# First-group scores over 128 rows, value products two blocks at a time, scores last in a slot

## The chip, the cores and the metric

The kernel runs on one core of one Trainium2 chip. The metric is the device time of one execution in microseconds (us); for several runs their median is given. A profile is one execution recorded by the hardware profiler. Engines are PE (TensorE matmul; its weight loads have a row of their own, PEld), DVE (VectorE), ACT (ScalarE), POOL (GpSimd) and SP (SyncE, which issues most DMAs).

## The reference

Two layers over a sequence of 512 rows of 1024 floats. Each layer normalises, projects to queries, keys and values of three dilated attention groups (8 heads of 64), pools, gates, merges, and ends with a SwiGLU FFN. What matters here is the attention:

```python
scores = jnp.einsum('bhnqd,bhnkd->bhnqk', qb, kw).astype(jnp.float32) * (Dh ** -0.5)
scores = scores - slopes.astype(jnp.float32)[:, None, None, None] * dist[None, None]
scores = jnp.where(valid, scores, -1e30)
lse = jax.nn.logsumexp(scores, axis=-1)
p = jnp.exp(scores - lse[..., None])
out = jnp.einsum('bhnqk,bhnkd->bhnqd', p.astype(vw.dtype), vw)
...
wts = jax.nn.softmax(jnp.stack(lses, axis=0), axis=0)
att = jnp.sum(wts[..., None].astype(x.dtype) * jnp.stack(outs, axis=0), axis=0)
```

Queries see keys at most 64 steps away; the three groups step by 1, 4 and 16 positions.

## The kernel before

Float32 products are made of float32r parts: a value is split into a high part (a rounded copy, made by ACT) and a low part (the difference, made by DVE), and `mm3` (L239 to L241) multiplies high by high, high by low and low by high. A projection (`proj`) is 24 such matmuls of 512 columns, over 8 blocks of the model width, into one bank of PSUM.

The attention is done for a pair of heads at a time (j = 0 to 3, in both layers, 8 attentions). `qk(l, j)` makes six projections q0, k0, q1, k1, q2, k2, and calls `slot()` before each of them. A slot runs what is due of earlier work: deferred functions, then one step of each attention that is open (`self.attn`, oldest first), then one step of the adaLN weights (`ada_run`, one weight load and one DVE product, L205). Attention j is opened when its six projections are done, so its steps run between the projections of j + 1; those of the last pair run between the gate projections (`gates`), where a slot stands ahead of 36 matmuls. All engines take their instructions in the order in which the code issues them; nothing is planned by due times. So what a slot issues stands ahead of the next projection in PE's queue, and ahead of that projection's eviction and of the next weight splits (L198 on ACT, L199 on DVE) in the other queues.

An attention works on four blocks. Blocks 0 and 1 are the first group, each of two tiles of 128 queries; blocks 2 and 3 hold the second and third group side by side. The steps are these functions:

- `scores(blk)`: into the two PSUM banks "s". For blocks 0 and 1 there are 8 matmuls of 256 columns. The query tile of a head holds the high part on its own 64 rows and the low part on the other 64; `ks[h]` holds the head's key high part on both halves of the rows. So L541 (128 rows) gives high by high and low by high in one matmul, and L542 (the 64 rows of the query's high part, with the key's low part in `ks[2]`, both heads in one tile) adds high by low. For blocks 2 and 3 `mm3` is used with 12 matmuls of 256 columns and 128 rows. Then for each of four pieces a DVE reduction (L559) adds the distance table and takes the minimum, and an ACT exponential (L563) with that minimum as bias gives the weights and their sum.
- `transposes(blk)`: transposes the weights on PE into a bank "pt" (L573 for blocks 0 and 1, eight; L583 for blocks 2 and 3, four, with a DVE transposition L586 for the other half) and copies them out, half by DVE (L575) and half by ACT (L577, L587).
- `values(blk)`: 16 matmuls of 128 columns (L607) into a bank "mm" that the two blocks of a group share.
- `exchange()`: two POOL DMAs (L611, L612) that bring the sums of the first group into the layout of the others. `weigh()` (first instruction L620, DVE) combines the sums, `spread()` transposes the weights (L633) and broadcasts them with POOL DMAs (L637, L640), `combine()` (DVE, L645, L646 and a split) closes the attention two slots later. So the combine of attention j falls into slot 1 of attention j + 1.

Slot by slot before: 0: scores(0). 1: scores(1), transposes(0). 2: scores(2), transposes(1), exchange, values(0). 3: scores(3), transposes(2), values(1). 4: transposes(3), values(2), weigh. 5: values(3), spread. 6: nothing. 7: combine.

`key_tiles` builds the key tiles of the first group: `padded` evicts the projection into a padded tile (ACT L457, DVE L458), `stacked` makes high parts (ACT L465) and low parts (DVE L467), and two POOL copies (L473, L474) fill the other halves of `ks[0]` and `ks[1]`.

Of the kernel before, what the change touches and what calls it, by code (L numbers as in the profile page):

```python
# [12 lines left out]
F32 = mybir.dt.float32  # L13
F32R = mybir.dt.float32r
# [14 lines left out]
P = 128  # L29
# [15 lines left out]
def slope(g, h):  # L45
    return 2.0 ** (-8.0 * (8 * g + h + 1) / 24.0)


class Net:
# [71 lines left out]
    def slot(self):  # L121
        due, keep = [], []
        for e in self.later:
            e[0] -= 1
            (due if e[0] <= 0 else keep).append(e)
        self.later = keep
        for e in due:
            e[1]()
        self.attn = [g for g in self.attn if next(g, True) is None]
        while self.ada:  # L130
            if next(self.ada[0], True) is None:
                break
            self.ada.pop(0)
# [10 lines left out]
        return self.sb.tile(shape, dt, tag=tag, name=self.name(tag), bufs=bufs)  # L144

    def g(self, shape=(P, 2, S), dt=F32):
        return self.t("g", list(shape), dt, 23)

    def bank(self, tag="mm"):
        return self.ps.tile([P, S], F32, tag=tag, name=self.name(tag), bufs={"mm": 4, "s": 2, "pt": 2}[tag])  # L150
# [299 lines left out]

    def padded(self, pb):
        nc = self.nc
        vp = self.t("kp", [P, 5, 8, 16], F32, 4)
        src = pb.rearrange("d (c u t) -> d t u c", c=16, u=8)
        nc.gpsimd.memset(vp[:, 0, 0:4], 0.0)
        nc.gpsimd.memset(vp[:, 4, 4:8], 0.0)
        nc.scalar.copy(vp[:, 0:4, 4:8], src[:, :, 0:4])  # L457
        nc.vector.tensor_copy(vp[:, 1:5, 0:4], src[:, :, 4:8])  # L458
        return vp
# [8 lines left out]

    def key_tiles(self, pb):
        full = self.padded(pb)  # L470
        ks = [self.t("kp", [P, 5, 8, 16], F32R, 4) for _ in range(3)]
        self.stacked(full, ks, (ks[2][0:64], ks[2][64:128]))
        self.nc.gpsimd.tensor_copy(ks[0][64:128], ks[0][0:64].bitcast(F32))  # L473
        self.nc.gpsimd.tensor_copy(ks[1][0:64], ks[1][64:128].bitcast(F32))  # L474
        return ks

    def query_tiles(self, pb, j):
# [43 lines left out]
    def attention(self, j, x, res):  # L521
        nc = self.nc
# [4 lines left out]
        def scores(blk):  # L527
            s, tt = divmod(blk, 2)
            pr[blk] = self.g([P, 2, 2, 256])
            sc = [self.bank("s") for _ in range(2)]  # L530
            for ti in range(2):
                t = 2 * tt + ti
                tk = slice(t * P, t * P + P)
                mm = nc.tensor.matmul
                for h in range(2):
                    if s == 0:
                        hs = slice(64 * h, 64 * h + 64)
                        o = sc[h][:, ti * 256 : ti * 256 + 256]
                        q, ks = x["q0"][:, h, tk], x["k0"]
                        k = lambda z: z[:, t : t + 2].rearrange("d b u c -> d (b u c)")  # L540
                        mm(o, lhsT=q, rhs=k(ks[h]), start=True, stop=False)  # L541
                        mm(o, lhsT=q[hs], rhs=k(ks[2])[hs], start=False, stop=True)  # L542
                    else:
                        o = sc[ti][:, h * 256 : h * 256 + 256]
                        q, ks = x[f"q{h + 1}"], x[f"k{h + 1}"]
                        k = lambda z: z[:, t].rearrange("d h k -> d (h k)")
                        self.mm3(o, q[:, 0, tk], q[:, 1, tk], k(ks[0]), k(ks[1]), True, True)
            for ti in range(2):
                t = 2 * tt + ti
                for h in range(2):  # L550
                    o = pr[blk][:, h, ti]
                    if s == 0:
                        tb, acc = (0 if t == 0 else 2 if t == 3 else 1), sta[:, t, h]
                        i0, i1, o2 = sc[h][:, ti * 256 : ti * 256 + 256], self.tab[:, tb], o
                    else:
                        acc = st[:, 1, t, h]
                        i0 = sc[ti].rearrange("q (g h k) -> q h g k", g=2, h=2)[:, h]
                        i1, o2 = (z.rearrange("q (g k) -> q g k", g=2) for z in (self.tab[:, 3], o))
                    nc.vector.tensor_tensor_reduce(  # L559
                        out=o2, in0=i0, in1=i1, op0=ALU.add, op1=ALU.min,  # L560
                        scale=-slope(s, 2 * j + h), scalar=3e38, accum_out=acc[:, 0:1],
                    )
                    nc.scalar.activation(o, o, AF.Exp, bias=acc[:, 0:1], scale=-1.0, accum_out=acc[:, 1:2])  # L563

        def transposes(blk):
            ptr[blk] = self.g([P, 2, S])
            if blk < 2:
                for h in range(2):
                    pt = self.bank("pt")
                    for ti in range(2):  # L570
                        for b in range(2):
                            c = (2 * ti + b) * P
                            nc.tensor.transpose(pt[:, c : c + P], pr[blk][:, h, ti, b * P : b * P + P], self.ident)  # L573
                    if h:
                        nc.vector.tensor_copy(ptr[blk][:, h], pt)  # L575
                    else:
                        nc.scalar.copy(ptr[blk][:, h], pt)  # L577
            else:
                pt = self.bank("pt")
                for h in range(2):  # L580
                    for ti in range(2):
                        c = (2 * h + ti) * P
                        nc.tensor.transpose(pt[:, c : c + P], pr[blk][:, h, ti, 0:P], self.ident)  # L583
                o = ptr[blk].rearrange("k h (t b q) -> k (h t) b q", t=2, b=2)
                i = pr[blk].rearrange("q h t (b k) -> q (h t) b k", b=2)
                nc.vector.transpose(o[:, :, 1], i[:, :, 1])  # L586
                nc.scalar.copy(o[:, :, 0], pt.rearrange("k (a q) -> k a q", a=4))  # L587

        def values(blk):
            s, tt = divmod(blk, 2)  # L590
            if tt == 0:
                pvs[s] = self.bank()
            pv = pvs[s]
            for ti in range(2):
                t = 2 * tt + ti
                for b in range(2):
                    for h in range(2):
                        hd = (2 * j + h) * HD
                        c = (2 * ti + b) * P
                        rhs = ptr[blk][:, h, c : c + P]  # L600
                        if s == 0:
                            o = pv[64 * h : 64 * h + 64].rearrange("d (c t) -> d t c", t=4)[:, t]
                            v = self.vs[(t + b) // 2][:, (t + b) % 2, hd : hd + HD]
                        else:
                            o = pv[64 * h : 64 * h + 64, t * P : t * P + P]
                            v = self.vb[t][:, b, hd : hd + HD]
                        nc.tensor.matmul(o, lhsT=v, rhs=rhs, start=b == 0, stop=b == 1)  # L607

        def exchange():
            d1 = self.dr.tile([P, 16], F32, tag="d1", name=self.name("d1"), bufs=2)  # L610
            nc.gpsimd.dma_start(out=d1, in_=sta.rearrange("q t h e -> q (t h e)"))  # L611
            nc.gpsimd.dma_start(out=st[:, 0].rearrange("q p h e -> q p (h e)"), in_=d1.rearrange("(p c) (t e) -> (c t) p e", p=4, t=4))  # L612
# [3 lines left out]
        def weigh():  # L616
            nmn = self.t("nmn", [P, 4, 2], F32, 2)
            es = self.t("es", [P, 2, 2, 4], F32, 2)
            z = self.t("z1", [P, 2, 4], F32, 2)
            nc.vector.tensor_tensor(nmn, st[:, 0, :, :, 0], st[:, 1, :, :, 0], op=ALU.min)  # L620
            for s in range(2):
                nc.vector.tensor_sub(wt[:, s], nmn.rearrange("q p h -> q h p"), st[:, s, :, :, 0].rearrange("q p h -> q h p"))
            nc.scalar.activation(wt, wt, AF.Exp)
            for s in range(2):
                nc.vector.tensor_mul(es[:, s], wt[:, s], st[:, s, :, :, 1].rearrange("q p h -> q h p"))
            nc.vector.tensor_add(z, es[:, 0], es[:, 1])
            nc.vector.reciprocal(z, z)
            for s in range(2):
                nc.vector.tensor_mul(wt[:, s], wt[:, s], z)
# [19 lines left out]
            res.append(at)  # L649

        for i in range(4):
            scores(i)
            if i >= 1:
                transposes(i - 1)
            if i == 2:
                exchange()
            if i >= 2:
                values(i - 2)
            yield
        transposes(3)  # L660
        values(2)
        weigh()
        yield
        values(3)
        wb = spread()
        yield
# [354 lines left out]

# [11 lines left out]
```

## Time and profile before

| | us |
|---|---|
| median of 3 runs | 1731.49 (1730.62 to 1733.04) |
| span of the profiled execution | 1732.1 |
| PE busy | 1688.3 |
| DVE busy | 965.5 |
| ACT busy | 658.7 |
| POOL busy | 351.1 |

The profiled execution has no other time of its own: its span, first to last instruction, is 1732.1 us, 0.6 over the median of the runs. PE's busy time is the union of its matmuls' lengths; matmuls overlap, so a busy PE can still be slower or faster in the distance from one start to the next, which the timeline shows. The attentions run from 158 to 360 us in layer 0 and from 1010 to 1211 us in layer 1.

### The profile page before, as it was taken

How to read it: one execution, taken by the hardware profiler on the slowest of the kernel's cores; microseconds unless marked ns; L12 is line 12 of the kernel's file. 1: busy time of each engine (PE TensorE's matmuls, PEld its weight loads, DVE VectorE, ACT ScalarE, POOL GpSimd, SP SyncE). 2: the span in 40 equal slices, each digit the busy share in tenths (PEclk: the TensorE clock that was granted, in tenths of full speed). 3: DMA queues.
4: the chain of work that ended last, by engine and by line, in shares of the span. 5: the costliest groups of instructions: out<-in, count | busy, mean ns of one | idle time of the engine just before them, and what ended most of it. 6: DMA issues, size and time to landing. Idle time of an engine off the chain costs nothing.

```text
span 1732.1 us, 21129 instructions
## 1 busy us (share of the span) xinstructions
PE 1688.3 (97%) x8162; PEld 1384.0 (80%) x8162; DVE 965.5 (56%) x1628; ACT 658.7 (38%) x1110; POOL 351.1 (20%) x317
## 2 busy tenths in 40 slices
PE   7899999999989999999999999999999999999998
PEld 5687788888779888888878887878887888888886
DVE  8657677545685554333473676764367844333435
ACT  4246444633443222221352554446234422222212
POOL 4301221002340000255330021120032400004540
PEclk9999999999999999999999999999999999999999
DMA  7524444332532555332522254452325344322331
GB/s 273 203 73 166 157 136 138 109 113 81 195 110 96 190 195 176 111 108 96 184 110 79 83 173 134 143 162 86 98 98 182 110 146 146 97 98 97 106 138 49
DMA packets 63799, 227.20 MB, mean 131 GB/s; under 512 B 7681, under 2 KB 8097, under 8 KB 63698
## 3 DMA queue, kind: packets, MB, share of 16 engines
q1 hardware_dynamic: 55296, 199.25, 33.9%
q0 software_dynamic: 8400, 26.59, 4.8%
q8 instruction: 64, 1.05, 0.3%
q14 instruction: 37, 0.30, 0.1%
q10 hardware_dynamic: 2, 0.00, 0.0%
HBM read 217.28 MB, written 8.54 MB: 130 GB/s over the span
## 4 chain that ended last, share of the span: by engine, by line
PE 90%; DVE 6%; ACT 2%; issue 1%; DMA 0%; POOL 0%; DVEq 0%
PE mm L239 21%; PE mm L241 20%; PE mm L240 20%; PE mm L775 8%; PE pt L775 5%; PE s L775 4%; PE mm L607 2%; PE mm L389 1%; DVE raw L205 1%; PE pt L389 1%; PE s L542 1%; PE s L541 1%; PE pt L573 1%; DVE nt L260 1%; DVE rs L264 1%
## 5 line engine op out<-in xcount | busy, mean ns | idle before, releaser
L239 PE MATMUL mm<-h,w 128*128 128x512 f32 (+1 forms) x1440 | 560.6, 389 | 0.0
L241 PE MATMUL mm<-h,w 128*128 128x512 f32 (+1 forms) x1440 | 554.6, 385 | 0.0
L240 PE MATMUL mm<-h,w 128*128 128x512 f32 (+1 forms) x1440 | 553.7, 385 | 0.0
L199 DVE TENSOR_TENSOR w<-raw,w 128x1024 fp32r<-128x1024 f32 x238 | 309.8, 1316 | 188.5 <-ACT w L198 188.5
L198 ACT CAST w<-raw 128x1024 fp32r<-128x1024 f32 x254 | 259.8, 1044 | 168.4 <-PE mm L775 141.7
L239 PEld LDWEIGHTS mm<-h,w 128*128 128x128 f32 x1440 | 270.6, 188 | 57.0 <-issue 3.8
L241 PEld LDWEIGHTS mm<-h,w 128*128 128x128 f32 x1440 | 270.6, 188 | 55.4
L240 PEld LDWEIGHTS mm<-h,w 128*128 128x128 f32 x1440 | 270.8, 188 | 52.4
L100 POOL TENSOR_TENSOR raw<-raw,g 128x1024 f32<-128x1024 f32 x60 | 158.2, 2648 | 375.0 <-DMA raw<-w_ffn_out 221.4
L198 ACT CAST g<-g 128x512 fp32r<-128x512 f32 x76 | 47.2, 621 | 336.7 <-DVE g L871 217.0
L775 PE MATMUL mm<-w,g 128*128 128x512 f32 x600 | 147.2, 395 | 0.0
L871 DVE TENSOR_TENSOR g<-g,mm 128x512 f32<-128x512 f32 x42 | 28.9, 688 | 211.4 <-PE mm L241 198.8
L775 PEld LDWEIGHTS mm<-w,g 128*128 128x128 f32 x600 | 112.6, 188 | 27.1
L205 DVE SCALAR_TENSOR_TENSOR raw<-raw,silc 128x1024 f32<-128x1024 f32 x96 | 132.2, 1384 | 1.6 <-DMA raw<-w_ada 1.6
L199 DVE TENSOR_TENSOR g<-g,g 128x512 fp32r<-128x512 f32 x76 | 61.9, 815 | 70.8 <-ACT g L198 70.8
L775 PE MATMUL s<-w,g 128*128 128x512 f32 x300 | 78.9, 403 | 2.1 <-ACT w L198 1.3
L775 PE MATMUL pt<-w,g 128*128 128x512 f32 x300 | 76.3, 395 | 0.0
L775 PEld LDWEIGHTS s<-w,g 128*128 128x128 f32 x300 | 57.5, 193 | 17.1 <-ACT w L198 1.8
L775 PEld LDWEIGHTS pt<-w,g 128*128 128x128 f32 x300 | 56.4, 188 | 13.6
L232 POOL DMA_DIRECT2D dg<-gr x4 | 2.1, 536 | 290.2 <-DVE gr L230 290.2
L473 POOL CAST kp<-kp 64x640 fp32r<-64x640 f32 x8 | 10.9, 1368 | 235.0 <-ACT kp L465 235.0
L870 ACT ACTIVATE g<-mm 128x512 f32<-128x512 f32 x42 | 25.2, 600 | 84.6 <-PE mm L241 84.6
(229 smaller groups left out, 2085.6 us busy)
## 6 DMA issues: line engine op xcount, KB each, us to landing
raw<-w_in SPq DMA_DIRECT2D x112, 512.0 KB, 3.3
raw<-w_ada SPq DMA_DIRECT2D x96, 512.0 KB, 4.3
raw<-w_ffn_in SPq DMA_DIRECT2D x88, 512.0 KB, 3.3
raw<-w_ffn_out SPq DMA_DIRECT2D x44, 512.0 KB, 3.2
raw<-w_o SPq DMA_DIRECT2D x16, 512.0 KB, 4.2
xs<-g POOLq DMA_DIRECT2D x12, 512.0 KB, 2.9
g<-xs POOLq DMA_DIRECT2D x12, 512.0 KB, 5.9
g<-d POOLq DMA_DIRECT2D x16, 256.0 KB, 5.6
```

The lines of the kernel that those rows point to most:

```text
L100: self.nc.gpsimd.tensor_mul(self.raws[i], self.raws[i], self.gate[info(i)][0])
L198: self.nc.scalar.copy(dst_hi, src)
L199: (self.nc.gpsimd if pool else self.nc.vector).tensor_sub(dst_lo, src, dst_hi.bitcast(F32))
L205: self.nc.vector.scalar_tensor_tensor(raw, raw, 1.0, self.silc, op0=ALU.mult, op1=ALU.mult, accum_out=self.mod[:, l, m : m + 1])
L239: mm(out, lhsT=whi, rhs=xhi, start=first, stop=False)
L240: mm(out, lhsT=whi, rhs=xlo, start=False, stop=False)
L241: mm(out, lhsT=wlo, rhs=xhi, start=False, stop=last)
L389: nc.tensor.matmul(pv[p, g], lhsT=hh[:, hi, tk], rhs=w[k][wi][:, c], start=k == 0 and i == 0, stop=k == KD - 1 and i == 2)
L607: nc.tensor.matmul(o, lhsT=v, rhs=rhs, start=b == 0, stop=b == 1)
L775: mm(acc[t][hf], lhsT=src[k][:, part, tk], rhs=wx[:, hf * S : hf * S + S], start=k == 0 and part == 0 and wi == 0, stop=k == K - 1 and par ...
L870: nc.scalar.activation(tmp[:, 0], pa, AF.Silu)
L871: nc.vector.tensor_mul(tmp[:, 1], tmp[:, 0], pb)
```

## The change

The key's low part gets a tile for each head (`ks[2]`, `ks[3]`), doubled on both halves of the rows by two more POOL copies, and the second score matmul of the first group contracts all 128 rows with it, so that low by low is added as well. In a slot the transpositions of block i - 1 are issued ahead of the scores of block i. The value products of blocks 0 and 1 are issued together in slot 3, behind scores(3), and those of blocks 2 and 3 in slot 5. The buffer counts of "kp" and "g" rise from 4 to 5 and from 23 to 24, and the descriptor scratch of POOL's DMAs, which was left at its default, is set to 8192 bytes.

```diff
--- before.py
+++ after.py
@@ -144,7 +144,7 @@
         return self.sb.tile(shape, dt, tag=tag, name=self.name(tag), bufs=bufs)
 
     def g(self, shape=(P, 2, S), dt=F32):
-        return self.t("g", list(shape), dt, 23)
+        return self.t("g", list(shape), dt, 24)
 
     def bank(self, tag="mm"):
         return self.ps.tile([P, S], F32, tag=tag, name=self.name(tag), bufs={"mm": 4, "s": 2, "pt": 2}[tag])
@@ -450,7 +450,7 @@
 
     def padded(self, pb):
         nc = self.nc
-        vp = self.t("kp", [P, 5, 8, 16], F32, 4)
+        vp = self.t("kp", [P, 5, 8, 16], F32, 5)
         src = pb.rearrange("d (c u t) -> d t u c", c=16, u=8)
         nc.gpsimd.memset(vp[:, 0, 0:4], 0.0)
         nc.gpsimd.memset(vp[:, 4, 4:8], 0.0)
@@ -468,10 +468,12 @@
 
     def key_tiles(self, pb):
         full = self.padded(pb)
-        ks = [self.t("kp", [P, 5, 8, 16], F32R, 4) for _ in range(3)]
-        self.stacked(full, ks, (ks[2][0:64], ks[2][64:128]))
-        self.nc.gpsimd.tensor_copy(ks[0][64:128], ks[0][0:64].bitcast(F32))
-        self.nc.gpsimd.tensor_copy(ks[1][0:64], ks[1][64:128].bitcast(F32))
+        ks = [self.t("kp", [P, 5, 8, 16], F32R, 5) for _ in range(4)]
+        self.stacked(full, ks, (ks[2][0:64], ks[3][64:128]))
+        for k in (ks[0], ks[2]):
+            self.nc.gpsimd.tensor_copy(k[64:128], k[0:64].bitcast(F32))
+        for k in (ks[1], ks[3]):
+            self.nc.gpsimd.tensor_copy(k[0:64], k[64:128].bitcast(F32))
         return ks
 
     def query_tiles(self, pb, j):
@@ -534,12 +536,11 @@
                 mm = nc.tensor.matmul
                 for h in range(2):
                     if s == 0:
-                        hs = slice(64 * h, 64 * h + 64)
                         o = sc[h][:, ti * 256 : ti * 256 + 256]
                         q, ks = x["q0"][:, h, tk], x["k0"]
                         k = lambda z: z[:, t : t + 2].rearrange("d b u c -> d (b u c)")
                         mm(o, lhsT=q, rhs=k(ks[h]), start=True, stop=False)
-                        mm(o, lhsT=q[hs], rhs=k(ks[2])[hs], start=False, stop=True)
+                        mm(o, lhsT=q, rhs=k(ks[2 + h]), start=False, stop=True)
                     else:
                         o = sc[ti][:, h * 256 : h * 256 + 256]
                         q, ks = x[f"q{h + 1}"], x[f"k{h + 1}"]
@@ -649,18 +650,19 @@
             res.append(at)
 
         for i in range(4):
-            scores(i)
             if i >= 1:
                 transposes(i - 1)
+            scores(i)
             if i == 2:
                 exchange()
-            if i >= 2:
-                values(i - 2)
+            if i == 3:
+                values(0)
+                values(1)
             yield
         transposes(3)
-        values(2)
         weigh()
         yield
+        values(2)
         values(3)
         wb = spread()
         yield
@@ -1021,7 +1023,7 @@
 
 def kernel(**inputs):
     arrays = layout(inputs)
-    nc = bacc.Bacc("TRN2", target_bir_lowering=False, num_devices=1)
+    nc = bacc.Bacc("TRN2", target_bir_lowering=False, num_devices=1, dynamic_dma_scratch_size=8192)
     a = {}
     for n, v in arrays.items():
         a[n] = nc.dram_tensor(n, v.shape, mybir.dt.from_np(v.dtype), kind="ExternalInput").ap()
```

## Rows read from the trace of the kernel before

**Rows 1.** The page: the span and the busy time, share and instructions of PE.

```profile
span 1732.1 us, 21129 instructions
...
PE 1688.3 (97%) x8162; PEld 1384.0 (80%) x8162; DVE 965.5 (56%) x1628; ACT 658.7 (38%) x1110; POOL 351.1 (20%) x317
```

**Rows 2.** Stretch in layer 1: length, busy PE, PEld, DVE, ACT, POOL; clock, DMA.

```profile
1060.00:1200.00 140.00, 140.00 (x779) 112.91 (x780) 90.23 (x213) 75.50 (x165) 22.68 (x39) 1.00 0.41 131
```

**Rows 3.** PE timeline, slot 0, first attention: start, length, line, operands, count.

```profile
158.00 0.39 PE L241 MATMUL mm<-h,w 128*128 128x512 f32 x1
158.23 0.28 PE L541 MATMUL s<-kp,g 128*128 128x256 f32 x1
158.44 0.38 PE L542 MATMUL s<-kp,g 64*128 64x256 f32 x1
...
160.62 0.50 PE L239 MATMUL mm<-h,w 128*128 128x512 f32 x1
160.96 0.39 PE L240 MATMUL mm<-h,w 128*128 128x512 f32 x1
```

**Rows 4.** PE timeline, slots 1 and 2 of the first attention.

```profile
166.20 0.28 PE L541 MATMUL s<-kp,g 128*128 128x256 f32 x1
...
168.60 1.09 PE L573 MATMUL pt<-ident,g 128*128 128x128 f32 x8
...
169.76 0.39 PE L240 MATMUL mm<-h,w 128*128 128x512 f32 x1
...
175.00 0.28 PE L239 MATMUL s<-g,g 128*128 128x256 f32 x1
...
176.43 1.03 PE L573 MATMUL pt<-ident,g 128*128 128x128 f32 x8
177.40 1.09 PE L607 MATMUL mm<-g,g 128*64 128x128 f32 x16
178.42 0.50 PE L239 MATMUL mm<-h,w 128*128 128x512 f32 x1
178.76 0.39 PE L240 MATMUL mm<-h,w 128*128 128x512 f32 x1
```

**Rows 5.** Instructions by line and shape: busy, mean ns, idle time before.

```profile
L607 PE MATMUL mm<-g,g 128*64 128x128 f32 x512 | 35.0, 279 | 0.0
```

**Rows 6.** PE timeline, second attentions, both layers: starts of slots.

```profile
214.38 0.28 PE L541 MATMUL s<-kp,g 128*128 128x256 f32 x1
...
223.18 0.28 PE L239 MATMUL s<-g,g 128*128 128x256 f32 x1
...
1066.02 0.28 PE L541 MATMUL s<-kp,g 128*128 128x256 f32 x1
```

**Rows 7.** DVE timeline, second attentions of both layers.

```profile
220.67 0.42 DVE L559 CUSTOM_DVE_ANT_0 g<-s,tab 128x256 f32<-128x256 f32 x1
...
222.04 0.69 DVE L575 COPY g<-pt 128x512 f32<-128x512 f32 x1
222.65 1.21 DVE L205 SCALAR_TENSOR_TENSOR raw<-raw,silc 128x1024 f32<-128x1024 f32 x1
...
244.20 0.12 DVE L620 TENSOR_TENSOR nmn<-st 128x8 f32<-128x8 f32 x1
...
1072.30 0.42 DVE L559 CUSTOM_DVE_ANT_0 g<-s,tab 128x256 f32<-128x256 f32 x1
```

**Rows 8.** ACT timeline: block 1, first attention; blocks 1, 2, second attention.

```profile
171.17 0.49 ACT L563 ACTIVATE g<-g,sta 128x256 f32<-128x256 f32 x1
...
223.11 0.56 ACT L577 COPY g<-pt 128x512 f32<-128x512 f32 x1
...
231.13 0.50 ACT L563 ACTIVATE g<-g,st 128x256 f32<-128x256 f32 x1
```

**Rows 9.** POOL timeline, second attention: a key copy, the exchange.

```profile
227.09 1.37 POOL L473 CAST kp<-kp 64x640 fp32r<-64x640 f32 x1 [18.36 <-ACT kp L465]
...
231.69 0.77 POOL L612 DMA_DIRECT2D st<-d  x1 [1.43 <-DMA d<-sta]
```

## The prediction, with its working

> **What bounds the kernel now.** I read the page first: TensorE (PE) is busy for 97% of a span of 1732.1 us [rows 1]. Then the table of stretches over the attention: PE busy 140.00 of 140 us at a granted clock of 1.00 (the 2.4 GHz level), VectorE (DVE) 90, ScalarE (ACT) 75, GpSimd (POOL) 23, DMA at 0.41 [rows 2]. So in this stage time is only what PE's queue takes, instruction by instruction, and every other engine is slack until PE has to wait for it. A full busy row doesn't say that PE runs at its peak: that is read from the distances between starts, in the timeline of PE. There the reader is to see that projection matmuls of 512 columns start 0.23 us apart (158.00 to 158.23), second-group score matmuls of 256 columns 0.12 us apart (twelve in 175.00 to 176.43), but first-group score matmuls, also of 256 columns, where 64-row ones alternate with 128-row ones, 0.30 us apart (eight in 158.23 to 160.62) [rows 3, 4].
>
> The stage consists of 8 attentions (4 head pairs, 2 layers). Each hangs its PE work on slots, one ahead of each projection of 24 matmuls. The rows are those of the first two attentions of layer 0; one is worked out and taken eight times.
>
> **Part 1: 128 rows in both score matmuls.** The edit changes 64 matmuls out of 64x256 into 128x256, so that all eight of a block have one shape. Before, the block of slot 0 takes 158.23 to 160.62 = 2.39 us, and the first projection matmul behind it takes 0.34 instead of 0.23: 2.50 in all [rows 3]. The block of slot 1 takes 166.20 to 168.60 = 2.40 [rows 4]. After, eight matmuls at the 0.119 of the second group (1.43/12, same columns, same types, all 128 rows) are 0.95. That is 1.55 + 1.45 = 3.00 us per attention. The trace has no block of this very kind; the bounds are 0.95 (as the second group) and 2.40 (the pitch stays), and I take the first because the shape is identical to it.
>
> A rule speaks against this edit: the Trainium skill, TensorE: Matmul & The Clock Gate, Part 3 (packing small matmuls), says that matmuls of few rows in distinct row groups run at the same time, so that widening them gives something up. By it two half-row matmuls would share one 0.12 step, and widening would cost 2 x 0.12 per block, 3.8 us over 16 blocks (estimate). The trace speaks against it here: 0.30 us from start to start, no pair shares a step [rows 3]. The Trainium skill, TensorEngine Tiling, Key Properties, has the other side: a change of tiling mode drains the engine.
>
> The doubled low part is 16 more POOL copies of the kind that runs ahead of the exchange; they and their effect are weighed as the last rival. The scores that read them come at least five slots later, and POOL is busy for 23 of 140 us [rows 2], so on PE's path I put them at nothing; without that cover each would cost its own length.
>
> **Part 2: value products two blocks together.** Sixteen value matmuls alone take 177.40 to 178.42 = 1.02; the first projection matmul behind takes 0.34 instead of 0.23 (178.42 to 178.76), and the last transposition before them, which starts 0.28 before the end of its group (176.43 + 1.03), has 0.21 to the first of them instead of 0.11: 1.23 [rows 4]. Inside the batch the pitch is (1.09 - 0.28)/15 = 0.054 [rows 4, 5], so sixteen right behind another sixteen cost 0.87. Merged twice per attention: 2 x 0.35 = 0.70 (0.36, rounded down). Where the batches go (slots 3 and 5 instead of 2 to 5) moves PE work only; what they read was copied at least a slot before.
>
> **Sum without waits:** 3.70 us per attention, 29.6 us in all.
>
> **Part 3: scores last in a slot.** In matmul time this is even: the eight transpositions and one projection matmul behind them take 168.60 to 169.76 = 1.16, which is 0.93 for the eight, and they cost that in either place [rows 4]. But a transposition of block i-1 needs its exponentials on ACT, which need the reduction on DVE. Before, 1.4 to 2.4 us of scores stood ahead of the transpositions as a cover. Now they stand first. And the copies that empty the transpositions (L575 on DVE, L577 on ACT) come ahead of the reductions and exponentials of block i in those two queues, where before they came behind; L575 puts the next instruction 0.61 us later (222.04 to 222.65) [rows 7].
>
> In slot 1 of the second attention (PE enters it at 214.38) DVE first has the combine of the attention before (L645, L646 and a split), so that the reductions begin at 220.67 and the last exponential ends at 223.11, where L577 follows it, which is 8.73 us after the slot's start; PE enters slot 2 at 223.18 [rows 6 to 8]. So the cover is just 0.07 us plus the 1.4 us of scores that the change takes away. After: PE would enter slot 2 at 8.80 - 1.45 = 7.35; the last exponential ends at 8.73 + 0.61 = 9.34; with 0.1 for the handover and the last two transpositions (0.22) the block ends at 9.67 instead of 7.35 + 0.93 = 8.28. **PE waits 1.4 us**, and behind the waiting transposition the scores of block 2 and the projection of q1 are queued.
>
> In slot 2 the lateness goes on. From the end of that exponential to the end of the last one of block 2 (231.13 + 0.50 = 231.63) DVE and ACT take 8.52 us without waiting for PE (split, key tiles, reductions, exponentials) [rows 8]. After: less 0.56 for L577, which has moved ahead, plus 0.61 for L575 ahead of the reductions: 9.34 + 8.57 = 17.9. PE enters slot 3 at 9.67 + 1.43 + 24 x 0.23 = 16.6 and would be through its four transpositions (half of 0.93) at 17.1; it is at 17.9 + 0.1 + 0.1 = 18.1. **Another 1.0 us.** In slots 3 and 4 the value products, now 32 in a row, give DVE and ACT their time back.
>
> Which attentions? The same lateness (reductions 6.28 us after the slot's start) stands in layer 1 (1066.02 to 1072.30) [rows 6, 7]; it is there in the second and third attention of each layer. The first has no combine before it: its last exponential of block 1 ends at 171.66, 5.46 after its slot began (166.20), with the copy 6.1, against 7.35 [rows 4, 8]. In the fourth the slots belong to the gates and are longer by twelve matmuls, 2.7 us. So 4 x 2.4 = 10 us. Bounds: zero, if the queues catch up; and if the first transposition already waits for all four exponentials, the block ends at 9.34 + 0.1 + 0.93 = 10.4 (2.1 late) and in slot 3 at 17.9 + 0.1 + 0.47 = 18.5 instead of 10.4 + 1.43 + 5.52 + 0.47 = 17.8 (0.7 late): 4 x 2.8 = 11; up to 6 x 2.8 = 17 if the two first attentions lose their 1.2 us too.
>
> The wider buffer counts (24 and 5) and the smaller descriptor scratch are in no term: they add no instruction.
>
> **How the numbers follow.** 29.6 - 10 = 19.6 us less PE time, with nothing behind the stage to eat it, since the stages after are also PE's. Profile: 1732.1 -> 1712.5; the median of the runs lies 0.6 below the profiled span (1731.49), so 1712.
>
> **Rivals.**
> *A, no wait:* DVE and ACT finish in time after all, and the whole 29.6 us come: 1702. For it: DVE idles a third of the stage. Against: the waits above are chains, not load. Chance 0.2.
> *B, wider waits:* the transpositions wait in the first attentions too, or the clock falls after the gaps; 17 us of waiting or more: 1719 to 1727. Chance 0.13.
> *C, the edit doesn't do what it says:* the 0.30 us has nothing to do with the 64 rows (it might be the same queries loaded twice, or the accumulation) and stays. Left are part 2's 5.6 us less the 1.0 us waits of slot 3's transpositions, four times: 1730. Against: the second group accumulates as well, at 0.12 [rows 4]. Chance 0.05. (The rule of packing above would put it here or worse.)
> *D, slower:* POOL's queue. The added copies stand ahead of the exchange of the softmax sums (its second DMA is issued at 231.69 in the second attention), and the smaller scratch may hold POOL's DMAs back. Whoever waits is the first instruction of the weighing (L620, at 244.20), and behind it in DVE's queue stand splits and reductions, on which PE waits in turn. From that issue to L620 are 12.5 us; two more copies of 1.37 take 2.7 of them [rows 7, 9]. So a landing of up to 9.8 us is hidden; each us beyond costs up to 8 us in all, the gain is gone at 9.8 + 19.6/8 = 12.2 us, and at 13.4 the kernel takes 1741. Against: POOL has 23 busy us in 140 [rows 2], and no row shows a DMA of it as late as that. Chance 0.04.
>
> Forecast 0.58 (1708 to 1718). The range 1702 to 1722 takes in A, the forecast and about half of B. A measurement of this kernel can tell about 0.2%, 3.5 us, from no change. Faster by more: forecast, A and B, and a little of C, 0.92; within: 0.04; slower: 0.04.
>
> **What would show it.** Right for part 1: first-group score matmuls start 0.12 us apart and the group of 64-row matmuls is gone. For part 2: 32 value matmuls in a row, pitch 0.054, in slots 3 and 5. For part 3: PE idle time ahead of the transpositions, released by ACT's exponentials, 1 to 1.5 us each, eight times, in the second and third attention only, and 3.7 us less from one attention's start to the next where there is none. Wrong: no idle time on PE there (A), idle time in all attentions or a granted clock below 1.00 in the stage (B), a pitch of 0.30 (C), or DVE waiting for a DMA ahead of L620 (D).

## The result, and the profile after

The changed kernel takes 1712.7 us (median of 4 runs, 1711.04 to 1713.66) against 1731.05 before: ratio 0.9886, 95% interval 0.9872 to 0.9900. Run again beside the last experiments it took 1710.2 against 1733.1: 0.9875 (0.9861 to 0.9888). Forecast was 1712 in a range of 1702 to 1722. The views below stand against the rows of before. The source lines behind the edits stand one or two further down, so L541 is now L542 and so on (L542 and L543 scores, L560 reductions, L564 exponentials, L574 and L584 transpositions, L608 value products, L613 the exchange's second DMA, L621 the weighing).

The page, against [rows 1], and the stretch of layer 1 that answers [rows 2] (busy PE, PEld, DVE, ACT, POOL, then clock and DMA):

```profile
span 1710.0 us, 21107 instructions
...
PE 1660.5 (97%) x8162; PEld 1373.8 (80%) x8162; DVE 968.5 (57%) x1628; ACT 659.8 (39%) x1110; POOL 362.2 (21%) x333
```

```profile
1040.00:1180.00 140.00, 136.39 (x800) 113.48 (x799) 91.97 (x214) 77.01 (x167) 28.60 (x48) 1.00 0.44 138
```

The same 97% on the page hides both halves of the story. In the stage (the stretch of the attentions) PE is idle for the first time, 3.6 us of 140, at an undiminished clock of 1.00, and the pace of its work is not in these rows.

PE's timeline in slot 0 of the first attention (start, length), against [rows 3]:

```profile
158.42 0.39 PE L241 MATMUL mm<-h,w 128*128 128x512 f32 x1
158.65 0.28 PE L542 MATMUL s<-kp,g 128*128 128x256 f32 x1
158.77 0.28 PE L543 MATMUL s<-kp,g 128*128 128x256 f32 x1
...
159.59 0.39 PE L239 MATMUL mm<-h,w 128*128 128x512 f32 x1
159.82 0.40 PE L240 MATMUL mm<-h,w 128*128 128x512 f32 x1
```

Read the distances: eight score matmuls in 158.65 to 159.59 = 0.94 us (0.95 was forecast) where 2.39 stood, and the projection behind them starts at its usual 0.23 instead of 0.34. Against [rows 4], the start of slot 1, then slots 2 and 3 of the same attention:

```profile
165.06 1.03 PE L574 MATMUL pt<-ident,g 128*128 128x128 f32 x8
...
172.35 1.03 PE L574 MATMUL pt<-ident,g 128*128 128x128 f32 x8
173.14 0.36 PE L239 MATMUL s<-g,g 128*128 128x256 f32 x1
...
180.47 0.36 PE L239 MATMUL s<-g,g 128*128 128x256 f32 x1
...
182.08 1.97 PE L608 MATMUL mm<-g,g 128*64 128x128 f32 x32
183.98 0.50 PE L239 MATMUL mm<-h,w 128*128 128x512 f32 x1
184.31 0.39 PE L240 MATMUL mm<-h,w 128*128 128x512 f32 x1
```

Thirty-two value products take 1.90 us to the next start (one batch alone took 1.02), and only one slow first projection matmul (0.33) is paid for both.

The second attention, against [rows 6]; in brackets the idle time before an instruction and what ended it:

```profile
209.46 1.04 PE L574 MATMUL pt<-ident,g 128*128 128x128 f32 x8
210.25 0.36 PE L542 MATMUL s<-kp,g 128*128 128x256 f32 x1
...
216.51 0.39 PE L241 MATMUL mm<-h,w 128*128 128x512 f32 x1
217.45 0.44 PE L574 MATMUL pt<-ident,g 128*128 128x128 f32 x2 [0.55 <-ACT g L564]
218.44 0.93 PE L574 MATMUL pt<-ident,g 128*128 128x128 f32 x6 [0.55 <-ACT g L564]
219.12 0.36 PE L239 MATMUL s<-g,g 128*128 128x256 f32 x1
...
226.21 0.33 PE L584 MATMUL pt<-ident,g 128*128 128x128 f32 x1
227.19 0.82 PE L584 MATMUL pt<-ident,g 128*128 128x128 f32 x3 [0.66 <-ACT g L564]
227.77 0.36 PE L239 MATMUL s<-g,g 128*128 128x256 f32 x1
```

Slot 1 starts at 209.46; in the first attention it is 7.29 us from there to the next slot (165.06 to 172.35) and the eight transpositions take 0.79 (172.35 to 173.14). So the block should end at 217.54 and ends at 219.12: 1.58 us late. The brackets show only 1.1 of it (twice 0.55), because a matmul's recorded length overlaps its neighbour's; distances between starts tell the loss. In slot 3 the four transpositions end at 227.77, 8.65 after 219.12; in the first attention it is 7.33 (173.14 to 180.47), so this is 1.3 us late. DVE and ACT in between, against [rows 7, 8]:

```profile
215.74 0.68 DVE L576 COPY g<-pt 128x512 f32<-128x512 f32 x1
216.34 0.42 DVE L560 CUSTOM_DVE_ANT_0 g<-s,tab 128x256 f32<-128x256 f32 x1
```

```profile
218.29 0.49 ACT L564 ACTIVATE g<-g,sta 128x256 f32<-128x256 f32 x1
...
227.05 0.49 ACT L564 ACTIVATE g<-g,st 128x256 f32<-128x256 f32 x1
```

The copy stands ahead of the reductions and puts them 0.60 us later (215.74 to 216.34). The last exponential of block 1 ends at 218.78, 9.32 after the slot's start (forecast 9.34), that of block 2 at 227.54, 18.08 after it (forecast 17.9). POOL's exchange and its reader, against [rows 9]:

```profile
228.32 0.77 POOL L613 DMA_DIRECT2D st<-d  x1 [1.43 <-DMA d<-sta]
```

```profile
240.32 0.12 DVE L621 TENSOR_TENSOR nmn<-st 128x8 f32<-128x8 f32 x1
```

12.0 us from the issue to L621, with nothing waited for.

What decides everything below is one number per attention, the distance from its first score matmul to that of the next, taken from PE's timeline. The starts of the second attention before, and of the second and third after:

```profile
206.41 0.28 PE L541 MATMUL s<-kp,g 128*128 128x256 f32 x1
```

```profile
203.04 0.28 PE L542 MATMUL s<-kp,g 128*128 128x256 f32 x1
...
250.33 0.28 PE L542 MATMUL s<-kp,g 128*128 128x256 f32 x1
```

With the first starts (158.23 and 158.65) that is 48.18 before, and 44.39 and 47.29 after. Both layers agree within 0.02 us, so layer 0 stands for both. The fourth attention lies among the gates; for it the distance to its last value product is given. The gain is the sum of the four against before, for two layers.

| kernel | median us | ratio to before (95%) | 1st | 2nd | 3rd | 4th | gain in the stage |
|---|---|---|---|---|---|---|---|
| before | | | 48.18 | 48.17 | 48.18 | 56.24 | |
| changed | 1712.7 | 0.9886 (0.9872 to 0.9900) | 44.39 | 47.29 | 47.29 | 52.45 | 18.7 |
| e1, rows only | 1710.9 | 0.9879 (0.9865 to 0.9892) | 45.10 | 45.45 | 45.45 | 53.14 | 23.3 |
| e2, value products only | 1726.4 | 0.9970 (0.9960 to 0.9981) | 47.51 | 47.53 | 47.54 | 55.56 | 5.3 |
| e3, order only | 1731.4 | 0.9997 (0.9988 to 1.0005) | 48.24 | 48.35 | 48.34 | 56.28 | -0.9 |
| e4, changed, scores first | 1705.6 | 0.9852 (0.9837 to 0.9867) | 44.43 | 45.15 | 45.16 | 52.44 | 27.2 |
| e5, changed, three combines later | 1705.5 | 0.9846 (0.9833 to 0.9860) | 44.39 | 44.39 | 44.39 | 54.07 | 27.1 |
| e6, scratch of 8192 bytes only | 1731.8 | 0.9996 (0.9987 to 1.0005) | 48.18 | 48.17 | 48.18 | 56.24 | 0.0 |
| e7, scores first and three combines later | 1705.0 | 0.9845 (0.9832 to 0.9858) | 44.43 | 44.43 | 44.43 | 53.62 | 27.7 |
| e8, half-row matmuls side by side | 1716.6 | 0.9904 (0.9889 to 0.9920) | 46.20 | 46.16 | 46.17 | 54.24 | 16.0 |
| e9, changed, two combines later | 1701.2 | 0.9820 (0.9807 to 0.9834) | 44.39 | 44.39 | 44.39 | 52.45 | 30.3 |
| e10, scores first and two combines later | 1704.7 | 0.9835 (0.9822 to 0.9849) | 44.43 | 44.43 | 44.43 | 52.44 | 30.1 |
| e11, changed again | 1710.2 | 0.9875 (0.9861 to 0.9888) | 44.39 | 47.29 | 47.29 | 52.45 | 18.7 |

The medians of before were 1731.05 (changed), 1731.81 (e1 to e4), 1731.62 (e5 to e8) and 1733.10 (e9 to e11). An attention of the changed kernel without waits is 3.79 us shorter than before, one with waits 0.88: the waits take 2.90 us in each of the second and third attentions.

### The profile page after: what moved, and what is told of

Its sections match the earlier page's. It is cut to its first block, busy times and chain, and to the rows that moved or that the text cites. A ratio compares the mean times of both kernels' runs of the same rounds, so it can differ in the third digit from the quotient of the medians.

```text
span 1710.0 us, 21107 instructions
## 1 busy us (share of the span) xinstructions
PE 1660.5 (97%) x8162; PEld 1373.8 (80%) x8162; DVE 968.5 (57%) x1628; ACT 659.8 (39%) x1110; POOL 362.2 (21%) x333
## 4 chain that ended last, share of the span: by engine, by line
PE 80%; DVE 11%; ACT 6%; issue 2%; DMA 0%; POOL 0%; DVEq 0%; ACTq 0%
PE mm L239 18%; PE mm L241 18%; PE mm L240 18%; PE mm L777 9%; PE pt L777 5%; PE s L777 4%; DVE raw L205 2%; PE mm L608 2%; DVE w L199 2%; PE mm L389 1%; PE pt L389 1%; ACT w L198 1%; ACT g L564 1%; DVE nt L260 1%; DVE rs L264 1%
## 5 line engine op out<-in xcount | busy, mean ns | idle before, releaser
L199 DVE TENSOR_TENSOR w<-raw,w 128x1024 fp32r<-128x1024 f32 x238 | 313.4, 1331 | 198.4 <-ACT w L198 198.4
L777 PEld LDWEIGHTS mm<-w,g 128*128 128x128 f32 x600 | 112.6, 188 | 27.2
L199 DVE TENSOR_TENSOR g<-g,g 128x512 fp32r<-128x512 f32 x76 | 67.3, 886 | 61.4 <-ACT g L198 61.4
L474 POOL CAST kp<-kp 64x640 fp32r<-64x640 f32 x16 | 21.0, 1341 | 244.8 <-ACT kp L465 176.6
```

The source lines that it names most:

```text
L199: (self.nc.gpsimd if pool else self.nc.vector).tensor_sub(dst_lo, src, dst_hi.bitcast(F32))
L777: mm(acc[t][hf], lhsT=src[k][:, part, tk], rhs=wx[:, hf * S : hf * S + S], start=k == 0 and part == 0 and wi == 0, stop=k == K - 1 and par ...
```

## The experiments

**One part at a time.** e1 takes from the change the key tiles and the second score matmul, and leaves the slots as before; e2 and e3 take the slots apart:

```diff
 # e1: against the kernel before
-mm(o, lhsT=q[hs], rhs=k(ks[2])[hs], start=False, stop=True)
+mm(o, lhsT=q, rhs=k(ks[2 + h]), start=False, stop=True)
 # e2: against the kernel before
-            if i >= 2:
-                values(i - 2)
+            if i == 3:
+                values(0)
+                values(1)
...
 # e3: against the kernel before
-            scores(i)
             if i >= 1:
                 transposes(i - 1)
+            scores(i)
```

(e1 also has the change's `key_tiles`, e2 the two late batches in slot 5; all three have the buffer counts and the scratch that they need.)

> The kernel before with part 1 alone (128 rows in both score matmuls of the first group, the low part doubled; the order in a slot and the value products as before). My theory, that the half-row matmuls cost by alternating with full-row ones: first-group score matmuls start 0.12 us apart, 3.0 us less per attention, and since the scores still stand ahead of the transpositions (about 1.4 us of cover) PE waits for no exponential: 24 us less than before, 1707. Rival C (the pitch has another cause): 1731, pitch still 0.30. Rival that the waits come from the shorter slots alone and not from the order: waits on PE ahead of transpositions as in the changed kernel, some 11 us of them, 1718.

> The kernel before with part 2 alone (value products of blocks 0 and 1 together in slot 3, of blocks 2 and 3 in slot 5). My theory: 0.70 us less per attention, 5.6 in all, no waits: 1725.5. Rival: the end of a batch costs nothing that isn't hidden, 1731.

> The kernel before with part 3 alone (transpositions of block i-1 ahead of scores of block i). My theory: in slots of the old length (8.80 us) the last exponential of block 1 comes 9.34 us after the slot's start, and the transpositions would be through at 8.80 + 0.93 = 9.73 anyhow, so the order alone costs PE next to nothing: 1731 to 1732. Rival, that the order costs its 10 to 12 us by itself because the copies stand ahead of the reductions: 1741 to 1743.

Measured: e1 1710.9, 20.9 us less than before (18.7 to 23.4 by its interval), and 23.3 in the stage. The first attention gives 3.08 of the 3.00 expected; the second and third give 2.73, and no wait for an exponential is left (the view of PE's waits names none in the stage). So the pitch came from the 64-row matmuls and rival C is out; how it came from them is asked by e8. The 0.35 us missing in two attentions are something else, which e4 shows. e2: 5.4 us in the runs, 0.64 to 0.68 an attention against 0.70. e3: nothing in the runs, 0.04 to 0.18 us an attention more in the trace, 0.9 in all. That is the interesting one: **the order that goes with 11.6 us of waits in the changed kernel is all but free in the old one.** Slots of 8.8 us leave the exponentials their time; slots of 7.3 don't. The waits belong to neither edit alone but to both together.

**Undoing the order in the changed kernel.**

```diff
 # e4: against the changed kernel
+            scores(i)
             if i >= 1:
                 transposes(i - 1)
-            scores(i)
```

> The changed kernel with part 3 undone (scores first in a slot, parts 1 and 2 kept). My theory: the waits of slot 2's transpositions (about 1.6 us in the changed kernel's second and third attentions) vanish, of those of slot 3 (1.3 us) some 0.3 stays: 1712.7 - 11.6 + 1.4 = 1702.5. Rival, that DVE and ACT are simply too slow for the shorter slots whatever the order: 1711 to 1713.

Measured 1705.6, 7.1 us under the changed kernel (8.5 in the stage), where 10.2 was expected. The transpositions wait for nothing any more, but the second and third attention still take 45.15 instead of 44.43. PE and DVE in slots 2 and 3 of the second attention of e4:

```profile
216.20 0.39 PE L241 MATMUL mm<-h,w 128*128 128x512 f32 x1
216.70 0.35 PE L239 MATMUL s<-g,g 128*128 128x256 f32 x1
...
224.33 0.39 PE L241 MATMUL mm<-h,w 128*128 128x512 f32 x1
224.87 0.36 PE L239 MATMUL s<-g,g 128*128 128x256 f32 x1 [0.15 <-DVE st L560]
```

```profile
216.12 0.42 DVE L560 CUSTOM_DVE_ANT_0 g<-s,tab 128x256 f32<-128x256 f32 x1
...
224.30 0.42 DVE L560 CUSTOM_DVE_ANT_0 g<-s,tab 128x256 f32<-128x256 f32 x1
```

From the projection's last start to the first score matmul it is 0.50 instead of 0.23 in slot 2 (in e1 too) and 0.54 in slot 3. The scores of block 2 write the two "s" banks that the reductions of block 1 still read; the third of them, the last on the first bank, ends at 216.54, and PE starts at 216.70. In slot 3 it is the second reduction of block 2, which ends at 224.72, and PE starts at 224.87. Behind each of the two late matmuls the next starts 0.07 us later than usual, so slots 2 and 3 give 0.72 us, all that is missing in e4, and slot 2 alone gives e1's 0.35. So with scores first the same lateness of DVE is met through the score banks rather than through the exponentials, only it costs 0.7 us an attention instead of 2.9. In my expectation the remaining 0.3 stood at slot 3's transpositions; it is in the banks of slots 2 and 3.

**Where the lateness comes from.** The combine of attention j stands ahead of the reductions of attention j + 1 in DVE's queue in slot 1. It can't be left out, but it can be moved, two slots later for some attentions:

```diff
 # e5: against the changed kernel (e7: against e4; e9, e10: the same with j < 2)
-        yield
-        yield
+        for _ in range(4 if j < 3 else 2):
+            yield
         combine(wb)
```

> The changed kernel with the combine of the first three attentions of a layer two slots later (slot 3 of the next attention instead of slot 1). My theory, that the waits come from the combine that stands ahead of the reductions in DVE's queue in slots 1 and 2: PE's waits ahead of the transpositions vanish in the second and third attentions (2.9 us each, 4 of them), an attention takes 44.4 us everywhere: 1712.7 - 11.6 = 1701. Rival, that the copies put ahead of the reductions are enough, or that the load only moves on: waits on PE ahead of the transpositions in slot 2, 3 or 4 of the same size, 1709 to 1713.

> The changed kernel with scores first in a slot and the combine of the first three attentions of a layer two slots later. In the kernel with scores first alone PE still waited 0.27 and 0.31 us for a score bank that late reductions held (45.15 instead of 44.44 us for the second and third attentions). My theory: with the combine out of the way that goes too, 44.4 us for each attention: 1705.6 - 2.8 = 1703, level with the kernel that has only the combine moved. Rival, that the bank is held whatever the combine does: 1705.5.

Measured: 44.39 us for each of the first three attentions in e5, 44.43 in e7, no wait of a transposition, no held score bank. So the combine ahead of the reductions is what makes DVE late; the copies ahead of them alone, which e5 keeps, cost PE nothing. But e5 takes 1705.5 and not 1701, and e7 1705.0 and not 1703. The fourth attention has become longer, 54.07 (e7: 53.62) instead of 52.45. The waits of PE in the stage of layer 0 in e5 (us, times, longest):

```profile
PE mm L608 <- ACT g L734: 1.6, 1, 1.6
```

The third attention's combine now falls into slot 3 of the fourth, and until then its two value banks stay occupied; the value products there wait for a bank that a sigmoid (L734) has to empty first. The expectation had missed that moving a reader also moves the release of what it reads. Leaving the third combine in its place should repair this:

> The changed kernel with the combine of only the first two attentions of a layer two slots later; the third's, which falls among the gates of the fourth attention, stays. With all three moved PE waited 1.6 us in the fourth attention of each layer for a bank of PSUM (value products behind a sigmoid). My theory: that wait goes too, 44.4 us from attention to attention and no wait of PE in the stage: 1705.5 - 3.2 = 1702. Rival, that the waits of the third attention's combine come back in the fourth: 1705 or more.

> The same with scores first in a slot (parts 1 and 2 of the change, part 3 undone, two combines later). My theory: with the combines out of the way the order in a slot has nothing left to cost or to bring: 1702, within 1 us of the kernel with the changed order.

> The changed kernel as it is, on the chip of the last two. My theory: 1712.5, and 10 us over them.

Measured: e9 1701.2, ratio 0.9820 to before, on the same chip 9 us under the changed kernel (1710.2, whose interval is clear of it). All attentions take 44.39 and 52.45, and PE waits for nothing in the stage. **e9 has the lowest median of the kernels here.** In e10 the stage is the same within 0.2 us, but the runs give 1704.7; the interval (0.9822 to 0.9849) overlaps that of e9 (0.9807 to 0.9834). In the two profiles the difference lies outside the stage: from the last value product of layer 0 to the first score of layer 1 it is 651.9 us in e10 and 649.1 in e9, a stretch that the two have in common instruction by instruction, and which runs from 646.9 to 651.9 over all the kernels here. Whether e10 is really slower is left open.

**The scratch.**

```diff
 # e6: against the kernel before
-num_devices=1)
+num_devices=1, dynamic_dma_scratch_size=8192)
```

> The kernel before with the descriptor scratch of POOL's DMAs at 8192 bytes and nothing else. My theory: no instruction and no wait changes, 1731.5. Rival D: POOL's DMAs are held back, landings of the exchange and of the weights' broadcast come later, 1734 or more.

Measured 0.9996 (0.9987 to 1.0005), every attention as before to 0.01 us. That part of rival D is out, and in the changed kernel L621 waited for nothing (above). e3 has the 24 buffers of "g" as well, and its time is that of before; the fifth buffer of "kp" was not tried by itself.

**What a 64-row matmul costs.** e8 keeps the 64-row matmuls and only puts two of them side by side, rows 0 to 63 and rows 64 to 127:

```diff
 # e8: against the kernel before
-                for h in range(2):
-                    mm(o, lhsT=q, rhs=k(ks[h]), start=True, stop=False)
-                    mm(o, lhsT=q[hs], rhs=k(ks[2])[hs], start=False, stop=True)
+                for part in range(2):
+                    for h in range(2):
+                        if part == 0:
+                            mm(o, lhsT=q, rhs=k(ks[h]), start=True, stop=False)
+                        else:
+                            mm(o, lhsT=q[hs], rhs=k(ks[2])[hs], start=False, stop=True)
```

> The kernel before with the order of the first group's score matmuls changed, nothing else: for each query tile first the two 128-row matmuls of both heads, then the two 64-row ones (rows 0 to 63, then rows 64 to 127). My theory, that the price is paid at each change between 128 and 64 rows (0.19 us over the 0.12 step): four changes a block instead of eight, a block takes 1.66 instead of 2.39, 0.73 x 16 = 11.7 us less, 1720. By the rule of the Trainium skill on row groups (TensorE: Matmul & The Clock Gate, Part 3) the two 64-row matmuls would in addition run at the same time, 0.12 us less for each pair, 1716. Rival, that a 64-row matmul is slow by itself (0.30 us each): within 3 us of before, 1729 to 1732.

Measured 1716.6, 15.1 us less than before, 16.0 in the stage: the number that my price of a change gives together with the Trainium skill's rule (TensorE: Matmul & The Clock Gate, Part 3: matmuls in distinct row groups run at the same time), not the 1720 of the price alone. PE's timeline in slot 0 of the first attention of e8, and the two score lines of its kernel (L543 and L545) by shape (busy us, mean ns):

```profile
158.41 0.40 PE L543 MATMUL s<-kp,g 128*128 128x256 f32 x2
158.74 0.38 PE L545 MATMUL s<-kp,g 64*128 64x256 f32 x2
159.05 0.50 PE L543 MATMUL s<-kp,g 128*128 128x256 f32 x2
159.48 0.38 PE L545 MATMUL s<-kp,g 64*128 64x256 f32 x2
159.79 0.49 PE L239 MATMUL mm<-h,w 128*128 128x512 f32 x1
```

```profile
L543 PE MATMUL s<-kp,g 128*128 128x256 f32 x64 | 14.4, 306 | 0.0
L545 PE MATMUL s<-kp,g 64*128 64x256 f32 x64 | 12.3, 381 | 0.0
```

The 64-row line of the kernel before:

```profile
L542 PE MATMUL s<-kp,g 64*128 64x256 f32 x64 | 24.4, 381 | 0.0
```

Two 64-row matmuls last 0.38 us from the first start to the last end, as long as one (381 ns each), and 64 of them fill 12.3 us: each pair runs at once. What is left is the price of each change of shape: 0.31 us from a half-row start to the next full-row one, where two full-row starts lie 0.12 apart. The full-row matmuls pay a part of it: the two behind a half-row pair take 0.43 us to the next pair (159.05 to 159.48), the two ahead of the first pair 0.33 (158.41 to 158.74). So a block takes 1.38 us; in full rows 0.94. Whether the 0.31 itself is all the change, or in part a 64-row matmul that is slower by itself, no run separates: none has several half-row pairs in a row.

## Why the prediction was right, step by step

- *PE bounds the stage; busy time hides its pace.* Held. All of the gain is in distances between starts.
- *Part 1, 3.00 us an attention.* Held: 3.08 in e1's first attention. The step chose the lower bound (0.95 a block) for its identical shape; it is 0.94. The Trainium skill's rule on row groups (TensorE: Matmul & The Clock Gate, Part 3) was put aside with "no pair shares a step". That was right for the half-row score matmuls of the kernel before, no two of which are neighbours, but not because the rule fails: e8 shows it at work as soon as they are. e8's order alone brings 16.0 of the 23.3 us that the widening brings.
- *Part 2, 0.70 an attention.* Held: 0.64 to 0.68 in e2. The pitch of 0.054 is a mean: in the trace of before, too, the value products start in pairs, the two heads' 7 ns apart, and 0.109 us from pair to pair.
- *Sum without waits, 29.6.* 30.3 by e9 (8 x 3.79).
- *Part 3, waits of 1.4 and 1.0 us in the second and third attention.* Right in place and releaser, a little small in size: 1.58 and 1.3. The exponentials came within 0.2 us of the worked times (9.32 for 9.34, 18.08 for 17.9), and the waiting block of slot 2 ended when it was worked out to end, 9.66 us after its slot's start for 9.67. What was too large is the time at which PE would have been through without a wait, taken at 8.28 and 8.08 by the first attention (7.29 + 0.79): the 0.93 taken for eight transpositions holds the slow matmul behind them, and the eight alone take 0.79. The sum of the waits is 11.6 instead of 4 x 2.4 = 9.6, which the forecast rounded to 10. Three things must meet for them, the shorter slots (e3: order alone all but free), the order (e4: undone, 0.7 of 2.9 stays) and the combine in slot 1 (e5 and e9: moved, none stays). No wait came behind slot 3; the value products given as the reason for slots 3 and 4 stand in slots 3 and 5.
- *Net 19.6:* 18.7 in the stage. The errors of the last two points, +0.7 and -1.6, cancel in part; the net is that near to the forecast partly by luck.
- *Rivals.* A (no wait) falls with the profile, though it is where e9 gets to. B: no wait in the first and fourth attentions, clock 1.00. C falls with e1. D: e6, and L621 without a wait.

The prediction has no term for the score banks. With scores first DVE's lateness stands there, so undoing the order doesn't give the whole of the waits back (e4).

## What to carry to other kernels

Look at the distance between starts, not at busy time, wherever full-row and part-row matmuls alternate: either give them one shape or put part-row ones of different row groups next to each other. When PE's work between two steps is cut by a sixth, redo the sum of the chain on the other engines that used to hide behind it; an order that costs nothing in long slots can cost more than a quarter of the gain in short ones (8.5 of 30.3 us, by e4 and e9). And before a step is put elsewhere to clear a queue, look at what it holds until it has run: moving three combines won 11.6 us of waits and lost 3.2 to occupied banks, moving two lost nothing.

## What the runs showed of the hardware

Two 64-row float32r matmuls in different row halves ran at the same time when they were neighbours (e8: 12.3 us for 64, 24.4 in the kernel before, where they were not); I had expected them one after the other. In the kernel before, where 64-row and 128-row matmuls alternate, a step takes about 0.19 us over the 0.12 of a full-row one, and this falls on the steps into a full-row matmul and into a half-row one alike. The edges of a batch of value products (128 rows, outputs on one half of the partitions) cost in the same way: in the kernel before 0.20 us instead of 0.11 into the batch, 0.20 out of it, and 0.34 instead of 0.23 at the projection's first step, so part 2 seems to save the same kind of price as part 1; no run tests that. The waits in the changed kernel, up to 1.6 us in a block of dense matmul work and eight of them, left the granted clock of the stage at 1.00. A descriptor scratch of 8192 bytes for POOL's DMAs in place of the default changed no time here.
